# A hybrid decoder layer on one core: mixer outputs loaded straight into the output projection's operand

## The chip, the cores and the metric

The kernel runs on one core of a Trainium2 chip. The metric is device time in microseconds (us). The engines are TensorE (PE, with its weight loads as PEld), VectorE (DVE), ScalarE (ACT), GpSimd (POOL) and SyncE (SP), whose queue issues nearly all DMAs.

## The reference

One layer over a sequence of 512 tokens of width 2048, in float32:

```python
h = _rmsnorm(x, norm_w[l])
p = h @ w_in[l]                       # 2048 x 7824
...
y_a = _rwkv7_mix(...)                 # 16 heads of 64: 1024 columns
y_b = _moba_mix(q_b, k_b, v_b, g_b)   # 4 heads of 128: 512 columns
y_c = _gla_mix(...)                   # 4 heads of 128: 512 columns
mix = jnp.concatenate([y_a, y_b, y_c], axis=-1)
x = x + mix @ w_out[l]                # 2048 x 2048
return _rmsnorm(x, final_norm_w)
```

## The kernel before

**Products in three parts.** Each float32 operand of a projection is split into a rounded high part and the rest: ScalarE copies it to `hi`, VectorE subtracts to get `lo`. A product is then three matmuls, `hi*hi`, `lo*hi` and `hi*lo`. The activations are held in 16 pairs of tiles, `hT[k]`, named `hhi0` to `hhi15` and `hlo0` to `hlo15`, each 128x512.

**The input projection** goes through 62 jobs (`wdad` to `mg3`), each of four units of 12 matmuls with 512 columns (the job `low` is one unit). Unit g of a job reads `hT[4g]` to `hT[4g+3]`. The last job, `mg3`, accumulates in bank `gb1`. Weights come in tiles of 256 KB through three buffers, `raw0` to `raw2`, and are split into four slots, `hi0` to `hi3` and `lo0` to `lo3`. A load may go into a raw buffer when VectorE has split what was in it.

**Side work** (the three mixers) is written as coroutines. `pump` resumes them between the matmuls of the projection by a clock that the program keeps while it is being written; `force` resumes them until a flag is set. Their small matmuls use the banks `sb0` to `sb3`, and their copies and sums stand in the queues of ScalarE and VectorE between the splits. Each finished mixer output is a 128x512 tile, a "mix"; there are 16, and each is written to its own DRAM tensor `mix0` to `mix15`.

**The output projection** has 64 units: four column blocks `cb` of 512 columns, and in each 16 blocks n of w_out, taken in the order `K_ORDER`. Unit (cb, n) multiplies the mix `K_ORDER[n]` by a 128x512 tile of w_out: four row groups `tb` of three matmuls, 12 in all. In the first column block the mixes have to come back from DRAM. Before, they stand in the list `items` between the w_out tiles: mix, w_out, mix, w_out. Each goes through a raw buffer of its own turn (`load`, L1067), and is split from there into `hT[n]` (`split`, L1107), which the input projection has finished with by then. Column blocks 1 to 3 load w_out alone.

The residual input `x` is loaded by `load_x` in four DMAs per column block, in the first three when block n = 8 begins. In the first column block, three row groups of blocks 0 and 1 are done before the fourth, since the fourth needs bank `gb1`, which VectorE must first empty (`f4<-gb1`).

Of the kernel before, what the change touches and what calls it, by code (L numbers as in the profile page):

```python
# [9 lines left out]
F32 = mybir.dt.float32  # L10
F32R = mybir.dt.float32r
I32 = mybir.dt.int32
AF = mybir.ActivationFunctionType
ALU = mybir.AluOpType
# [3 lines left out]
KT = D // 128  # L18
# [31 lines left out]


JOBS = [(n, first_column(n)) for n in ORDER.split()]
N_FIRST = 3
NGB = 4
SKEW = (0, 5, 12, 30)
# [37 lines left out]
def tile_hybrid(ctx: ExitStack, tc: tile.TileContext, x, xT, wu, wlow, wout, par, cst, w2a2_d, aup_d, fw, out):  # L93
    nc = tc.nc
# [179 lines left out]
    Xd = dram.tile([32, 32, 32], F32, name="Xd")  # L274
    mixd = [dram.tile([128, S], F32, name=f"mix{k}") for k in range(KT)]
    mix_ready = [False] * KT


    sides = []
# [429 lines left out]
    def group_norm(q):  # L709
        yield flag(f"y{q}")  # L710
        ysq = ARBf[:, 0:1024]
        y = Yqf.rearrange("p (g n) -> p g n", n=C)
        red(gn[:, 0], y)
        ts(gn[:, 0], gn[:, 0], 1.0 / C, None, ALU.mult)
        tt(y, y, gn[:, 0, :, None].to_broadcast([128, 16, C]), ALU.subtract)
        yield None
        act(ysq, Yqf, AF.Square)
        yield None
        red(gn[:, 1], ysq.rearrange("p (g n) -> p g n", n=C))
        yield None  # L720
        yield from rsqrt(gn[:, 1], gn[:, 2], 1.0 / C, GN_EPS)
        tt(y, y, gn[:, 2, :, None].to_broadcast([128, 16, C]), ALU.mult)
        yield None
        for j in range(2):
            pr = 2 * q + j
            b = yield from bank()
            for cp in range(4):
                tr(sbk[b][:, cp * 128:(cp + 1) * 128], Yq[:, cp, j * 128:(j + 1) * 128])
            u = ARBf[:, 1024 + S * j:1024 + S * j + S]
            act(u, sbk[b], AF.Identity, bias=col(P_LB, pr), scale=col(P_LW, pr))  # L730
            release(b)
            yield None
            tt(u, u, bv[j], ALU.add)
            yield flag(f"ga{pr}")
            tt(u, u, sgt[j], ALU.mult)
            yield None
            dma(mixd[pr], u, nc.sync)
            mix_ready[pr] = True
            yield None
        flags[f"finish{q}"] = True  # L740

# [60 lines left out]
    def gla(g):  # L802
# [114 lines left out]
        for i in range(2):  # L917
            h = 2 * g + i
            sg = fb[5 + i]
            yield flag(f"gg{h}")  # L920
            b = yield from bank()
            for w in range(4):
                tr(sbk[b][:, w * 128:(w + 1) * 128], t3(fo[i])[:, w])
            stt(fo[i], sbk[b], col(P_GN), sg, ALU.mult, ALU.mult)
            release(b)
            yield None
            dma(mixd[12 + h], fo[i], nc.sync)
            mix_ready[12 + h] = True
            yield None


    def moba(h):
        sc = 128 ** -0.5
        yield from evac(f"mq{h}", fb[0])
        yield from evac(f"mk{h}", fb[1])
        n_done = [0]

        def window(w, p, pT):

            n = 128 * (w + 1)  # L940
            sm = small[:, 32 + 4 * w:36 + 4 * w]
            b = yield from bank()
            mm(sbk[b][:, :n], fb[0][:, 128 * w:128 * w + 128], fb[1][:, :n])
            yield None
            tt(sbk[b][:, n - 128:n], sbk[b][:, n - 128:n], causal, ALU.add)
            red(sm[:, 0:1], sbk[b][:, :n], ALU.max)
            ts(sm[:, 1:2], sm[:, 0:1], -sc, None, ALU.mult)
            yield None
            act(p[:, :n], sbk[b][:, :n], AF.Exp, bias=sm[:, 1:2], scale=sc, accum=sm[:, 2:3])
            release(b)  # L950
            yield None
            ck.add("dve", 0.1)
            nc.vector.reciprocal(sm[:, 3:4], sm[:, 2:3])
            ts(p[:, :n], p[:, :n], sm[:, 3:4], None, ALU.mult)
            yield None
            b = yield from bank()
            for i in range(w + 1):
                tr(sbk[b][:, 128 * i:128 * i + 128], p[:, 128 * i:128 * i + 128])
            act(pT[:, :n], sbk[b][:, :n], AF.Copy)
            release(b)  # L960
            yield flag(f"mv{h}")
            b = yield from bank()
            for i in range(w + 1):
                mm(sbk[b][:, 0:128], fb[3][:, 128 * i:128 * i + 128], pT[:, 128 * i:128 * i + 128],
                   start=(i == 0), stop=(i == w))
            vcopy(fb[7][:, 128 * w:128 * w + 128], sbk[b][:, 0:128])
            release(b)
            yield None
            n_done[0] += 1

        def windows(ws, p, pT):
            for w in ws:
                yield from window(w, p, pT)

        spawn(f"m{h} even", windows((0, 2), fb[5], fb[6]))
        yield from evac(f"mv{h}", fb[2])
        b = yield from bank()
        for w in range(4):
            tr(sbk[b][:, w * 128:(w + 1) * 128], fb[2][:, w * 128:(w + 1) * 128])
        act(fb[3], sbk[b], AF.Copy)  # L980
        release(b)
        yield None
        flags[f"mv{h}"] = True
        spawn(f"m{h} odd", windows((1, 3), fb[2], att.rearrange("p a t -> p (a t)")))
        yield lambda: n_done[0] == 4
        yield flag(f"mg{h}")
        tt(fb[7], fb[7], fb[4], ALU.mult)
        yield None
        dma(mixd[8 + h], fb[7], nc.sync)
        mix_ready[8 + h] = True  # L990
        yield None

    def moba_gate(h):
# [13 lines left out]
            flags[f"moba{h}"] = True  # L1007


    K_ORDER = [0, 1, 12, 13, 2, 3, 14, 15, 8, 9, 4, 5, 10, 6, 7, 11]  # L1010
    items, units = [], []
    index = {n: i for i, (n, _) in enumerate(JOBS)}
    tile_no = {n: i for i, n in enumerate([n for n, _ in JOBS if n != "low"])}
# [18 lines left out]
    n_in = len(units)  # L1032
    for cb in range(4):
        for n in range(KT):
            if cb == 0:
                items.append(("mix", n))
            add_unit(("out", cb, n))
    item_of, slot_of, nth, last_in_slot = {}, {}, 0, []
    for i, (kind, n) in enumerate(items):
        if kind == "w":  # L1040
            item_of[n] = i
        if kind in ("w", "mix"):
            slot_of[i] = nth
            nth += 1
            last_in_slot.append(i)
# [21 lines left out]
    def load(i):  # L1067
        kind, n = items[i]
        dep = 0.0
        if kind == "x":  # L1070
            o, src = xraw[n], xT[128 * n:128 * n + 128]
        else:
            slot = slot_of[i]
            o = raws[slot % NRAW]
            if slot >= NRAW:
                dep = split_end[last_in_slot[slot - NRAW]]
            if kind == "mix":
                k = K_ORDER[n]
                force(lambda: mix_ready[k], f"mix {k}")
                src = mixd[k]  # L1080
            else:
                u = units[n]
                if u[0] == "in":
                    src = wu[tile_no[u[1]] * 4 + u[2]]
                elif u[0] == "low":
                    o, src = o[:, 0:KT * 16], wlow
                else:
                    k = K_ORDER[u[2]]
                    src = wout[128 * k:128 * k + 128, 512 * u[1]:512 * u[1] + 512]
        nc.sync.dma_start(o, src)  # L1090
        ck.t["dma"] = max(ck.t["dma"], dep) + 0.75
        load_end[i] = ck.t["dma"] + 2.0

    def square(n, r):

        if n == 0:
            act(fb[0], r, AF.Square)
        else:
            e = act(fb[1 + n % 3], r, AF.Square)
            late_adds.append((n, e))  # L1100
        while late_adds and (len(late_adds) > 2 or n == KT - 1):
            m, e = late_adds.pop(0)
            ck.add("pool", 1.25, e + 0.2)
            nc.gpsimd.tensor_tensor(fb[0], fb[0], fb[1 + m % 3], op=ALU.add)  # L1104
            squares[0] = m + 1

    def split(i):  # L1107
        kind, n = items[i]
# [11 lines left out]
        if kind == "w" and units[n][0] == "low":  # L1120
            v = wl2[:, 0:KT * 32].rearrange("p (k s n) -> p k s n", k=KT, s=2)
            rv = r[:, 0:KT * 16].rearrange("p (k n) -> p k n", k=KT)
            hi, lo, r = v[:, :, 0], v[:, :, 1], rv
        elif kind == "mix":
            hi, lo = hT[n]
        else:
            hi, lo = slot(n)
        e = act(hi, r, AF.Copy, dep=dep)
# [67 lines left out]
    for u in range(n_in):  # L1196
# [22 lines left out]
        unit_end[u] = ck.t["pe"]  # L1219
        if g == 3 or kind == "low":  # L1220
            jobs[n].done, jobs[n].end = True, ck.t["pe"]


    ys = [BKf, BKtf, VSf, ARBf]
# [19 lines left out]

    oldest = [gb[(n_started + i) % NGB] for i in range(NGB)]
    waiting = [bank_job[(n_started + i) % NGB] for i in range(NGB)]
    for cb in range(3):
        banks = oldest if cb % 2 == 0 else sbk
        order = [(n, tb) for n in range(KT) for tb in range(4)]
# [3 lines left out]
        for i, (n, tb) in enumerate(order):  # L1253
            u = n_in + cb * KT + n
            if tb == 0 and not (cb == 0 and n == 1):
                begin(u)
            if cb == 0 and n == 0:
                wait_free(waiting[tb])
            if n == 8 and tb == 0:
                if cb == 0:  # L1260
                    force(lambda: not sides, "side work")
                    nc.gpsimd.dma_start(fwt, fw.rearrange("(o d) -> o d", o=1).to_broadcast([128, D]))
# [97 lines left out]
```

## Time and profile before

| what | value |
|---|---|
| median of 3 runs | 1063.88 us (1063.74 to 1065.58) |
| profiled execution, device time | 1066.24 us |
| its span, first to last instruction | 1064.5 us |
| TensorE busy | 1039.1 us, 98% |
| VectorE, ScalarE busy | 63%, 42% |
| mean granted TensorE clock | 0.992 |

The profiled execution is one more execution, taken with the profiler on. Its device time is 1.74 us more than its span. In the trace `gb` and `sb` are the two groups of PSUM banks, and buffer numbers are left out: `hi` is any of the four slots, `raw` any of the three buffers, `f` any of eight work tiles.

### The profile page before, as it was taken

The page shows a single profiled execution, that of the slowest core. Times are in us where ns is not written, and L with a number is a line of the kernel's source. Part 1 is how long each engine was busy: PE and PEld are TensorE (multiplying, and loading weights), DVE is VectorE, ACT ScalarE, POOL GpSimd, SP SyncE. Part 2 cuts the span into 40 slices and gives each one's busy share as a digit, 9 for nine tenths or more (in the row PEclk, how much of TensorE's full clock was granted, in tenths as well). Part 3 has the DMA queues.
Part 4 walks back from the last instruction along what each step waited for, and adds up shares of the span by engine and source line. Part 5 has one row for each costly group of instructions (what it writes and reads, how often), then busy time and mean ns, then how long its engine had stood idle before and what let it go on. Part 6 is the DMA issues. An engine that isn't in the chain of part 4 may idle for free.

```text
span 1064.5 us, 16752 instructions
## 1 busy us (share of the span) xinstructions
PE 1039.1 (98%) x6376; PEld 819.9 (77%) x6376; DVE 667.2 (63%) x1346; ACT 443.7 (42%) x789; POOL 71.9 (7%) x73
## 2 busy tenths in 40 slices
PE   7799999999999999999999999999999999899996
PEld 5587888767788887778888777888877778688885
DVE  6646659657757775576788665667955654434343
ACT  6464543342554443235534513545322354423333
POOL 4500000000100000010000001000000100102020
PEclk9899999999999999999999999999999999999999
DMA  7232333412232342223333222333341345543534
GB/s 250 94 96 79 91 93 95 110 55 84 80 114 81 100 116 77 77 75 114 97 97 104 75 70 71 98 90 101 104 105 50 83 156 165 162 158 97 161 119 158
DMA packets 80400, 111.87 MB, mean 105 GB/s; under 512 B 28208, under 2 KB 29424, under 8 KB 80192
## 3 DMA queue, kind: packets, MB, share of 16 engines
q1 hardware_dynamic: 80176, 109.76, 34.9%
q8 instruction: 50, 0.82, 0.3%
q0 software_dynamic: 144, 1.05, 0.3%
q14 instruction: 30, 0.25, 0.1%
HBM read 98.62 MB, written 12.16 MB: 104 GB/s over the span
## 4 chain that ended last, share of the span: by engine, by line
PE 90%; DMA 3%; ACT 2%; POOL 2%; issue 2%; DVE 1%; SPq 0%; ACTq 0%; POOLq 0%
PE gb L120 68%; PE sb L116 11%; PE sb L120 9%; PE sb L125 2%; DMA raw<-in_wout_dram 2%; POOL f L1104 2%; DMA raw<-mix 1%; ACT hi L173 1%; ACT hhi L173 1%; DMA BK<-Xd 0%; DVE hlo L133 0%; DMA raw<-in_wu_dram 0%; DVE lo L133 0%; ACT f L173 0%; SPq L1243 0%
## 5 line engine op out<-in xcount | busy, mean ns | idle before, releaser
L120 PE MATMUL gb<-hhi,hi 128*128 128x512 f32 x976 | 403.9, 414 | 5.7 <-ACT hi L173 5.7
L120 PE MATMUL gb<-hhi,lo 128*128 128x512 f32 x976 | 383.3, 393 | 1.0 <-DVE lo L133 1.0
L120 PE MATMUL gb<-hlo,hi 128*128 128x512 f32 x976 | 382.9, 392 | 0.3 <-DVE hlo L139 0.3
L173 ACT ACTIVATE hi<-raw 128x512 fp32r<-128x512 f32 x296 | 186.0, 630 | 391.0 <-PE gb L120 273.3
L133 DVE TENSOR_TENSOR lo<-raw,hi 128x512 fp32r<-128x512 f32 x296 | 212.6, 722 | 209.3 <-ACT hi L173 201.9
L120 PEld LDWEIGHTS gb<-hhi,hi 128*128 128x128 f32 x976 | 184.2, 189 | 49.9 <-ACT hi L173 5.9
L120 PEld LDWEIGHTS gb<-hhi,lo 128*128 128x128 f32 x976 | 184.1, 189 | 42.2 <-DVE lo L133 2.1
L120 PEld LDWEIGHTS gb<-hlo,hi 128*128 128x128 f32 x976 | 184.6, 189 | 34.5 <-DVE hlo L139 1.4
L133 DVE TENSOR_TENSOR scr<-scr 64x30 f32<-64x30 f32 (+14 forms) x240 | 77.5, 323 | 7.2
L120 PE MATMUL gb<-hi,hhi 128*128 128x512 f32 x128 | 50.9, 398 | 2.6 <-ACT hi L173 2.6
L120 PE MATMUL gb<-lo,hhi 128*128 128x512 f32 x128 | 50.7, 396 | 0.2 <-DVE lo L133 0.2
L120 PE MATMUL gb<-hi,hlo 128*128 128x512 f32 x128 | 50.3, 393 | 0.0
L173 ACT ACT_TABLE_LOAD x34 | 43.6, 1283 | 1.0 <-DVE VS L153 0.4
L153 DVE COPY VS<-sb 64x128 f32<-64x128 f32 x64 | 18.5, 289 | 32.7 <-PE sb L116 31.7
L363 POOL TENSOR_TENSOR gn<-gn,mhalf 128x16 f32<-128x16 f32 (+1 forms) x5 | 13.0, 2603 | 309.5 <-DVE gn L149 309.5
L173 ACT ACTIVATE Lt<-sb 64x256 f32<-64x256 f32 (+1 forms) x64 | 19.3, 326 | 33.1 <-PE sb L116 30.5
L173 ACT ACTIVATE f<-sb 64x256 f32<-64x256 f32 (+3 forms) x52 | 17.2, 362 | 35.6 <-PE sb L125 19.2
L120 PE MATMUL sb<-lo,hhi 128*128 128x512 f32 x80 | 31.2, 390 | 0.0
L120 PE MATMUL sb<-hi,hhi 128*128 128x512 f32 x80 | 31.2, 389 | 0.0
L120 PE MATMUL sb<-hi,hlo 128*128 128x512 f32 x80 | 31.2, 389 | 0.0
L120 PEld LDWEIGHTS gb<-hi,hhi 128*128 128x128 f32 x128 | 24.4, 191 | 8.3 <-ACT hi L173 3.3
L120 PE MATMUL sb<-late,hhi 128*128 128x512 f32 x96 | 30.2, 395 | 0.0
(228 smaller groups left out, 1142.9 us busy)
## 6 DMA issues: line engine op xcount, KB each, us to landing
raw<-in_wu_dram SPq DMA_DIRECT2D x244, 256.0 KB
raw<-in_wout_dram SPq DMA_DIRECT2D x64, 256.0 KB
raw<-mix SPq DMA_DIRECT2D x16, 256.0 KB
f<-in_x_dram SPq DMA_DIRECT2D x16, 256.0 KB
Ld<-Lt SPq DMA_DIRECT2D x4, 512.0 KB
mix<-f SPq DMA_DIRECT2D x8, 256.0 KB
mix<-ARB SPq DMA_DIRECT2D x8, 256.0 KB
AW<-in_xT_dram SPq DMA_DIRECT2D x6, 256.0 KB
```

Of the source, the lines that this page charges most:

```text
L116: nc.tensor.matmul(o, l, r, start=start, stop=stop)
L120: nc.tensor.matmul(o, l, r, start=start, stop=stop)
L125: nc.tensor.transpose(o, i, ident[:k, :k])
L133: nc.vector.tensor_tensor(o, a, b, op=op)
L153: nc.vector.tensor_copy(o, a)
L173: nc.scalar.activation(o, a, f, **kw)
L363: nc.gpsimd.tensor_tensor(r, v, mhalf[:, 0:n], op=ALU.pow)
L1104: nc.gpsimd.tensor_tensor(fb[0], fb[0], fb[1 + m % 3], op=ALU.add)
```

## The change

- Mixes leave the list `items` and no longer use raw buffers. A mix is loaded from DRAM straight into the tile `hlo[n]` of the operand (`fetch_mixes`); `place_mixes` then copies it to `hhi[n]` on ScalarE and subtracts in place on VectorE.
- The loads are written into SP's queue earlier. After each of the four units of the last input job, up to four more mixes are fetched, as far as they are ready, and the rest during the first column block.
- A mix that is finished after the input projection was written (here mix 11, the last) does not go to DRAM: it is split from the tile it was computed in (`mixed`).
- `load_x` of the first column block may wait until the side work is done, up to block 13.

```diff
+    def mixed(k, u):
+        if projected_all[0]:
+            hi, lo = hT[K_ORDER.index(k)]
+            act(hi, u, AF.Copy)
+            tt(lo, u, hi.bitcast(F32), ALU.subtract)
+            direct.add(k)
+        else:
+            dma(mixd[k], u, nc.sync)
+        mix_ready[k] = True
...
-            dma(mixd[pr], u, nc.sync)
-            mix_ready[pr] = True
+            mixed(pr, u)
...
     for cb in range(4):
         for n in range(KT):
-            if cb == 0:
-                items.append(("mix", n))
             add_unit(("out", cb, n))
...
-            if kind == "mix":
-                k = K_ORDER[n]
-                force(lambda: mix_ready[k], f"mix {k}")
-                src = mixd[k]
...
+    def fetch_mixes(upto):
+        while fetched[0] < upto and mix_ready[K_ORDER[fetched[0]]]:
+            n = fetched[0]
+            if K_ORDER[n] not in direct:
+                nc.sync.dma_start(hT[n][1].bitcast(F32), mixd[K_ORDER[n]])
+                ck.t["dma"] = max(ck.t["dma"], ck.t["pe"]) + 0.75
+                mix_end[n] = ck.t["dma"] + 2.0
+            fetched[0] += 1
+
+    def place_mixes(must, may):
+        cur, ck.cur = ck.cur, None
+        while placed[0] < KT:
+            n = placed[0]
+            k = K_ORDER[n]
+            if n <= must:
+                force(lambda: mix_ready[k], f"mix {k}")
+                fetch_mixes(n + 1)
+            elif n > may or n >= fetched[0] or mix_end.get(n, 0.0) > ck.t["pe"]:
+                break
+            if k not in direct:
+                hi, lo = hT[n]
+                e = act(hi, lo.bitcast(F32), AF.Copy, dep=mix_end[n])
+                tt(lo, lo.bitcast(F32), hi.bitcast(F32), ALU.subtract, dep=e + 0.2)
+            placed[0] += 1
+        ck.cur = cur
...
-        elif kind == "mix":
-            hi, lo = hT[n]
...
+        if u >= n_in - 4:
+            fetch_mixes(4 * g + 4)
+            place_mixes(-1, KT)
+    projected_all[0] = True
...
                 begin(u)
+                if cb == 0:
+                    fetch_mixes(KT)
+                    place_mixes(n + 1, n + 6)
...
-            if n == 8 and tb == 0:
+            if tb == 0 and n >= 8 and x_loaded < cb + 1 and (cb or not sides or n == KT - 3):
+                x_loaded += 1
```

The instructions of all engines stand as before up to the last input units; the differences lie between there and the end of the first column block. Two places follow.

The queue of SP at the end of the input projection, before: `raw<-in_wout` rows are w_out blocks 0, 1, 2, 3 and 4, `raw<-mix` the mixes between them, and `mix<-ARB` two mixes written out.

```order
L1090 DMA raw0_97<-in_wout_dram 128x512
L179 DMA mix6_180<-ARB_127 128x512
L1090 DMA raw1_98<-mix1_175 128x512
L1090 DMA raw2_99<-in_wout_dram 128x512
L1090 DMA raw0_97<-mix12_186 128x512
L1090 DMA raw1_98<-in_wout_dram 128x512
L1090 DMA raw2_99<-mix13_187 128x512
L1090 DMA raw0_97<-in_wout_dram 128x512
L179 DMA mix7_181<-ARB_127 128x512
L1090 DMA raw1_98<-mix2_176 128x512
L1090 DMA raw2_99<-in_wout_dram 128x512
```

The same place after the change; the first row is w_out block 1, block 0 standing just ahead of it in the place of the first mix.

```order
L1093 DMA raw0_97<-in_wout_dram 128x512
L181 DMA mix6_180<-ARB_127 128x512
L1117 DMA hlo0_66<-mix0_174 128x512
L1117 DMA hlo1_68<-mix1_175 128x512
L1117 DMA hlo2_70<-mix12_186 128x512
L1117 DMA hlo3_72<-mix13_187 128x512
L1093 DMA raw1_98<-in_wout_dram 128x512
L1117 DMA hlo4_74<-mix2_176 128x512
L1117 DMA hlo5_76<-mix3_177 128x512
L1117 DMA hlo6_78<-mix14_188 128x512
L1117 DMA hlo7_80<-mix15_189 128x512
L1093 DMA raw2_99<-in_wout_dram 128x512
```

Four mixes now stand ahead of w_out block 2 (`raw1`) and eight ahead of block 3 (`raw2`), where before each block had one more mix ahead of it. Behind the last row come four mixes, block 4, the write of mix 7, three mixes, and blocks 5 to 13; the loads of `x` stand behind block 13.

ScalarE over the first output blocks, before: `f2`, `f6` and `att` are steps of the last MoBA head, `hi` rows are splits of w_out, `hhi` rows of mixes.

```order
L173 ACTIVATE hi2_102<-raw2_99 128x512
L173 ACTIVATE f2_151,small_160<-sb1_166,small_160 128x512
L173 ACTIVATE hhi2_69<-raw0_97 128x512
L173 ACTIVATE hi3_103<-raw1_98 128x512
L173 ACTIVATE hhi3_71<-raw2_99 128x512
L173 ACTIVATE hi0_100<-raw0_97 128x512
L173 ACTIVATE f6_155<-sb3_168 128x384
L173 ACTIVATE att_157<-sb0_165 128x512
```

The same place after the change.

```order
L175 ACTIVATE f2_151,small_160<-sb1_166,small_160 128x512
L175 ACTIVATE hhi1_67<-hlo1_68 128x512
L175 ACTIVATE hhi2_69<-hlo2_70 128x512
L175 ACTIVATE hhi3_71<-hlo3_72 128x512
L175 ACTIVATE hi3_103<-raw1_98 128x512
L175 ACTIVATE f6_155<-sb3_168 128x384
L175 ACTIVATE hhi4_73<-hlo4_74 128x512
L175 ACTIVATE hhi5_75<-hlo5_76 128x512
L175 ACTIVATE hhi6_77<-hlo6_78 128x512
L175 ACTIVATE hhi7_79<-hlo7_80 128x512
L175 ACTIVATE hi0_100<-raw2_99 128x512
L175 ACTIVATE att_157<-sb2_167 128x512
```

`f6` moved ahead of the split of w_out block 3 (`hi0`), and `att` now stands behind it and behind four more mixes.

## Rows read from the trace of the kernel before

**Rows 1.** page, part 1: busy time of each engine
```profile
PE 1039.1 (98%) x6376; PEld 819.9 (77%) x6376; DVE 667.2 (63%) x1346; ACT 443.7 (42%) x789; POOL 71.9 (7%) x73
```

**Rows 2.** waits of TensorE, whole span: us in total, times, longest
```profile
PE gb L120 <- ACT hi L173: 8.4, 2, 5.7
...
PE sb L116 <- ACT f L173: 1.0, 1, 1.0
```

**Rows 3.** chain that ended last, 840 to the end: start us, us, what
```profile
866.04 3.36 DMA raw<-in_wout_dram
...
872.62 3.93 DMA raw<-in_wout_dram
...
877.28 0.39 ACT f L173
...
905.29 7.38 DMA raw<-mix
...
924.47 43.52 PE sb L120 x192
967.99 43.52 PE gb L120 x192
```

**Rows 4.** timeline of TensorE, 858 to 925: start us, us, instruction, count
```profile
858.75 0.48 PE L120 MATMUL gb<-hhi,hi 128*128 128x512 f32 x1
...
871.65 0.39 PE L120 MATMUL gb<-hi,hhi 128*128 128x512 f32 x1
...
876.29 0.40 PE L120 MATMUL gb<-hi,hlo 128*128 128x512 f32 x1
...
877.72 0.94 PE L116 MATMUL sb<-f,f 128*128 128x128 f32 x6 [1.03 <-ACT f L173]
...
907.73 0.39 PE L120 MATMUL gb<-hi,hlo 128*128 128x512 f32 x1
...
911.10 0.39 PE L120 MATMUL gb<-hi,hlo 128*128 128x512 f32 x1
...
914.10 0.80 PE L120 MATMUL gb<-hi,hhi 128*128 128x512 f32 x1 [2.61 <-ACT hi L173]
...
917.54 0.39 PE L120 MATMUL gb<-lo,hhi 128*128 128x512 f32 x1
...
924.31 0.39 PE L120 MATMUL sb<-hi,hhi 128*128 128x512 f32 x1
```

**Rows 5.** stretches: us, busy (x), PEclk, DMA share, GB/s
```profile
905.70:908.10 2.40, 2.40 (x12) 1.81 (x10) 0.82 (x2) 0.63 (x1) 0.00 (x0) 1.00 0.88 237
908.10:910.50 2.40, 2.17 (x10) 1.56 (x10) 0.54 (x1) 0.00 (x0) 0.00 (x0) 1.00 0.96 335
914.10:917.50 3.40, 3.40 (x7) 2.43 (x8) 1.27 (x2) 0.50 (x1) 0.00 (x0) 0.50 0.60 172
```

**Rows 6.** timeline of SP's queue: start us, us, issue, count
```profile
856.81 0.33 SPq L1090 DMA_DIRECT2D raw<-in_wout_dram  x1
...
903.35 1.84 SPq L1243 DMA_DIRECT2D f<-in_x_dram  x4
...
945.31 1.85 SPq L1243 DMA_DIRECT2D f<-in_x_dram  x4
```

**Rows 7.** timeline of ScalarE: start us, us, instruction, count
```profile
862.84 1.28 ACT L173 ACT_TABLE_LOAD   x1
...
946.27 0.63 ACT L173 ACTIVATE hi<-raw 128x512 fp32r<-128x512 f32 x1 [2.09 <-PE sb L120]
```

**Rows 8.** page, part 5: the copies into hi, all of them
```profile
L173 ACT ACTIVATE hi<-raw 128x512 fp32r<-128x512 f32 x296 | 186.0, 630 | 391.0 <-PE gb L120 273.3
```

**Rows 9.** timeline of VectorE, around 866
```profile
865.93 0.69 DVE L133 TENSOR_TENSOR lo<-raw,hi 128x512 fp32r<-128x512 f32 x1
866.53 0.69 DVE L133 TENSOR_TENSOR ARB<-ARB,bv 128x512 f32<-128x512 f32 x1
867.13 0.29 DVE L133 TENSOR_TENSOR sb<-sb,consts 128x128 f32<-128x128 f32 x1
```

More of the change, by code (lines that the diff above doesn't have):

```diff
@@ L52 @@
 JOBS = [(n, first_column(n)) for n in ORDER.split()]
+K_ORDER = [0, 1, 12, 13, 2, 3, 14, 15, 8, 9, 4, 5, 10, 6, 7, 11]
 N_FIRST = 3
@@ L276, in tile_hybrid @@
     mix_ready = [False] * KT
+    projected_all, direct = [False], set()
+    def mixed(k, u):
[7 more added lines that the diff above has]
+        mix_ready[k] = True
     sides = []
@@ L926, in gla @@
             yield None
-            dma(mixd[12 + h], fo[i], nc.sync)
-            mix_ready[12 + h] = True
+            mixed(12 + h, fo[i])
             yield None
@@ L988, in moba @@
         yield None
-        dma(mixd[8 + h], fb[7], nc.sync)
-        mix_ready[8 + h] = True
+        mixed(8 + h, fb[7])
         yield None
@@ L1007, in others @@
             flags[f"moba{h}"] = True
-    K_ORDER = [0, 1, 12, 13, 2, 3, 14, 15, 8, 9, 4, 5, 10, 6, 7, 11]
     items, units = [], []
@@ L1041, in tile_hybrid @@
             item_of[n] = i
-        if kind in ("w", "mix"):
+        if kind == "w":
             slot_of[i] = nth
@@ L1076, in load @@
                 dep = split_end[last_in_slot[slot - NRAW]]
-            if kind == "mix":
-                k = K_ORDER[n]
-                force(lambda: mix_ready[k], f"mix {k}")
-                src = mixd[k]
-            else:
[L1082 to L1089, printed above, removed]
+            u = units[n]
+            if u[0] == "in":
+                src = wu[tile_no[u[1]] * 4 + u[2]]
+            elif u[0] == "low":
+                o, src = o[:, 0:KT * 16], wlow
+            else:
+                k = K_ORDER[u[2]]
+                src = wout[128 * k:128 * k + 128, 512 * u[1]:512 * u[1] + 512]
         nc.sync.dma_start(o, src)
@@ L1105, in square @@
             squares[0] = m + 1
+    mix_end, fetched, placed = {}, [0], [0]
+    def fetch_mixes(upto):
[22 more added lines that the diff above has]
+        ck.cur = cur
     def split(i):
@@ L1246, in tile_hybrid @@
     waiting = [bank_job[(n_started + i) % NGB] for i in range(NGB)]
+    x_loaded = 0
     for cb in range(3):
```

## The prediction, on record before the run

> **What bounds the kernel now.** I read the page first: TensorE is busy for 98% of the span [rows 1]. That alone doesn't say that nothing is to be had, because busy time there is modelled and holds slow matmuls too. The view of waits gives what is left: matmuls into `gb` waited 8.4 us for ScalarE's copies in two places, the longest 5.7, so the other about 2.7; and one side step waited 1.0 us for ScalarE [rows 2]. The 5.7 us lie at the start of the kernel, where nothing is changed. The chain of waits tells where the others are. In its last part TensorE goes on without a break, 192 matmuls in 43.52 us and again 192 in 43.52 us [rows 3], which is column blocks 1 and 2 of the output projection: 0.2267 us a matmul. The first column block has the same 192 matmuls, and in the timeline it lasts from 871.65 to 924.31, 52.66 us [rows 4]. So 9.14 us of it are not projection. That is the stage the change touches, and everything behind it is bound by TensorE, so what is won there reaches the end one to one.
>
> From the timeline [rows 4] those 9.14 us come apart as follows, each as the distance of two starts less 0.2267 us for each matmul between them.
> - 876.29 to 877.72: 1.43 less 0.23, **1.20 us**, waiting for ScalarE's `f6`.
> - 907.73 to 911.10: 3.37 less 12 matmuls (2.72), **0.65 us**.
> - 911.10 to 914.10: 3.00 less 0.23, **2.77 us**, waiting for a split of w_out by ScalarE.
> - 914.10 to 917.54: seven matmuls (1.59) took 3.44, **1.85 us** more. The granted clock is 0.50 in this stretch [rows 5], that is the 1.2 GHz level; TensorE had stood still just before.
> - The rest, 2.67 us, are 21 small side matmuls and their restarts. They stay.
>
> Sum of the four: 6.47 us. What caused them is in the chain [rows 3]. A split of w_out waited until 876.6 for a load issued at 872.62 that took 3.93 us, and `f6` stood behind that split on ScalarE until 877.28. At 905.29 a mix was loaded that took 7.38 us, against 3.36 us for a load at 866.04; just ahead of it in the queue stand the four loads of `x`, from 903.35 [rows 6]. While they ran, the DMA engines were busy for 0.88 and 0.96 of the time at 237 and 335 GB/s [rows 5]. Three raw buffers serve two loads for each block of 2.72 us (12 matmuls), so a late load can't be covered.
>
> **The change, part by part.**
>
> *Splits.* The same 16 copies and 16 subtractions remain, from `hlo` instead of `raw`. A subtraction in place isn't new: `ARB<-ARB,bv` takes 0.69 us as `lo<-raw,hi` does, and both let the next start 0.60 us later [rows 9]. Cost nothing. One write and one read of 256 KB (mix 11) go; they were off the path: nothing.
>
> *Raw buffers.* They now carry w_out alone, one load for each block, as in column blocks 1 to 3. There four loads of `x` stand in the queue too, at 945.31 [rows 6], and the next split waits 2.09 us for TensorE and not for a DMA [rows 7], while TensorE keeps its 43.52 us. So a 7.38 us landing behind `x` is hidden in this form, and the 0.65, 2.77 and, if the clock fell because of the pause, the 1.85 us go.
>
> *The mix loads* have a new wait. Each goes into an `hlo` that the last input job still reads. That job starts at 858.75 and the output at 871.65 [rows 4], so its four units begin some 3.2 us apart, and four mixes become free in each: up to about 862, 865, 868.5 and 871.5. SP's queue works in order, so w_out blocks 2, 3 and 4 stand behind them and leave at about 862.5, 866 and 869. Block 3 left at 872.62 before, so it is 6 us earlier in spite of the queue. How soon SP goes on after a matmul isn't in the trace; the nearest, 0.02 to 0.1 us between steps of the chain, is lost in these roundings, and even 1 us for all would be covered (below).
>
> The Trainium skill (DMA: Bandwidth & Descriptors, section Anatomy of one DMA — SWDGE (gpsimd) path) speaks against such loads: it says that the DMA engines never wait for a semaphore, the issuing sequencer does, before it dispatches. By that rule every w_out load is held for the mixes ahead of it. The sum already counts on that order, so by the rule it is the same, and the chance of rival 4 hangs on it; no row of before shows such a wait in this stage.
>
> *Transfers.* From 859 to 866 ten loads of 256 KB go out. At 237 to 335 GB/s [rows 5] each takes 0.8 to 1.1 us, so with 3.36 us for the first and nine more behind it, block 3, the tenth, lands between 869.5 and 872.5; if nothing is in the way, at 869.4. Block 4, with 15 transfers ahead since 859, lands by 874 to 879 and is wanted at about 882.
>
> *Is it in time?* ScalarE: a table load at 862.84 takes 1.28 us [rows 7], then come the SiLU of a gate, one split, a second table load and `f5`, to about 867; behind them six copies, `f2`, `f6`, five copies and `att`. At 0.63 us each [rows 8], an upper bound since they overlap, `f6` ends at about 872.2 and `hi0` of block 3 at about 875.3, `att` at 876. TensorE wants `f6` when nine matmuls of the output are done, about 874, and `att` after 15 matmuls and some 1.2 us of side work, about 876.7. Both are in time; the slack is 1.8 and 0.7 us, or over 1 us with overlap. Block 3 may land 2.5 us later than the worst above before it holds up `att`. VectorE: from 868 to the emptying of `gb1` about 13 rows at 0.60 [rows 9], done at about 877; wanted by the fourth row group at about 878.3. So the 1.20 us go too. Had this cover gone, the loss would be what is late, one to one.
>
> *The last mixes.* Mix 7 is written and read back in SP's queue, and its read waits for the write: 3.4 to 7.4 us by the loads [rows 3]. Blocks 5 and 6 stand behind it. Block 5 then leaves at 874 to 878, lands by 882, and is wanted at 887. Nothing.
>
> *Moved in the order:* `load_x` still comes at block 8, since the side work is done by then. Three transposes stand a few matmuls earlier: nothing.
>
> **Sum.** 6.47 us less about 0.3 for short waits that I can't place, 6.2 us. Of the profiled execution: 1066.24 to 1060.0, span 1064.5 to 1058.3. The median of the runs shown is 2.36 us below the profiled execution. I take the same 6.2 us off it: **1057.7 us**.
>
> **The rivals.**
> 1. *A part stays or comes back in the first five blocks* (ScalarE and VectorE are packed there, with 0.7 to 1.4 us to spare by my reckoning). One of the four terms stays, 0.65 to 2.8 us: 1058.5 to 1060.5. Against it: the splits of w_out no longer wait for loads. Chance 0.22.
> 2. *The pause was smaller without the profiler.* The 2.36 us between profile and median may lie in these stalls; then only about 4.1 us are to be had: 1059.8. Nothing in the trace tells. Chance 0.10.
> 3. *The load of `x` still stalls*: 2.77 and 1.85 us stay, since it was the burst and not the double use of the buffers: gain 1.6 to 1.85, 1062.1, no measurable change. Against it: column block 1, where the same burst costs nothing [rows 6, 7]. Chance 0.06.
> 4. *Slower: SP's queue is held by the mix loads.* If block 3 lands after 875, `att` and with it TensorE wait, one to one, and the clock falls again for about 1.85 us. It decides against the change when it costs more than 6.2 and 2.1 us: block 3 landing after about 881.5, 15 us after it was issued. The longest landing in this stage is 7.38 us [rows 3]. It would give 1066 and more. Chance 0.06.
>
> **How the numbers follow.** The forecast, all four stalls gone, has 0.56; it gives 1056.7 to 1058.7. About 0.2%, 2.1 us, is what a measurement of this kernel can tell from no change, so the border is 1061.75. Forecast and rivals 1 and 2 are faster: 0.88. Rival 3 is the same: 0.06; rival 4 slower: 0.06. The range from 1056.4 to 1061.2 holds the forecast and rivals 1 and 2, and leaves out rivals 3 and 4 and a little of each end.
>
> **What would show it.** The first column block would last about 46.2 us instead of 52.66, with no wait of a `gb` matmul there and no stretch of clock 0.50 in it. SP should issue mix loads from 859 to 872 and block 3 at about 866. ScalarE's `hi` rows behind block 4 should wait for TensorE, not for DMA. Right in time but wrong in mechanism: the wait stays and the clock does not fall. The prediction is wrong if `att` or the emptying of `gb1` holds TensorE by more than 2 us at 876 to 879, if a low clock comes at another place, or if the stalls don't exist outside the profile.

## The result and the profile after

The changed kernel took **1058.98 us** (median of 6 runs, 1058.08 to 1059.79); before, measured beside it, took 1064.73 us (1063.74 to 1065.85, 6 runs). The ratio is **0.9948, interval 0.9938 to 0.9959**: faster by 5.75 us, inside the range and 1.3 us above the forecast. Measured once more (below), the gain was 3.84 us. The profiled execution of after took 1058.42 us.

Page, span, part 1, and of part 5 one group of matmuls of the output projection:

```profile
span 1056.7 us, 16747 instructions
...
PE 1035.9 (98%) x6376; PEld 819.5 (78%) x6376; DVE 666.3 (63%) x1346; ACT 442.9 (42%) x789; POOL 71.9 (7%) x73
...
L122 PE MATMUL gb<-hi,hhi 128*128 128x512 f32 x128 | 50.0, 391 | 0.0
```

As many matmuls as in [rows 1], and the share of busy time says nothing, as before. The last number of the third row is what counts: no `gb<-hi,hhi` matmul waits any more. Waits of TensorE, in total, times, longest:

```profile
PE sb L118 <- POOL f L1107: 6.0, 1, 6.0
PE gb L122 <- ACT hi L175: 5.8, 1, 5.8
PE gb L122 <- DVE lo L135: 0.5, 1, 0.5
```

Of the waits in [rows 2] only the 5.7 us at the start of the kernel are left (5.8 here). The 6.0 us for GpSimd lie there too; the same view of before has them, with 6.0, and [rows 2] doesn't show that row. Chain of waits, 845 to the end, and then two stretches (us, busy of PE, PEld, DVE, ACT, POOL, PEclk, DMA share, GB/s):

```profile
870.16 2.77 PE gb L122 x12
872.93 0.67 PE sb L118 x6
...
876.30 40.17 PE gb L122 x177
916.47 43.52 PE sb L122 x192
959.99 43.52 PE gb L122 x192
```

```profile
860.00:870.00 10.00, 10.00 (x48) 7.88 (x46) 6.87 (x16) 8.96 (x15) 0.00 (x0) 1.00 0.88 265
870.00:916.00 46.00, 46.00 (x214) 38.37 (x213) 22.68 (x39) 19.48 (x33) 0.00 (x0) 1.00 0.49 162
```

All the `DMA raw<-` pieces of [rows 3] are gone from this part of the chain, and TensorE goes through column block 0 without a break at clock 1.00. Its first matmul starts at 870.70 and that of column block 1 at 916.31: 45.61 us, against 52.66 [rows 4]. SP's queue:

```profile
858.21 4.36 SPq L1117 DMA_DIRECT2D hlo<-mix  x4
862.67 0.38 SPq L1093 DMA_DIRECT2D raw<-in_wout_dram  x1
863.14 2.03 SPq L1117 DMA_DIRECT2D hlo<-mix  x4
865.26 0.38 SPq L1093 DMA_DIRECT2D raw<-in_wout_dram  x1
865.74 2.44 SPq L1117 DMA_DIRECT2D hlo<-mix  x4
868.73 0.33 SPq L1093 DMA_DIRECT2D raw<-in_wout_dram  x1
869.41 0.32 SPq L181 DMA_DIRECT2D mix<-ARB  x1
870.09 4.97 SPq L1117 DMA_DIRECT2D hlo<-mix  x3
875.15 18.59 SPq L1093 DMA_DIRECT2D raw<-in_wout_dram  x9
893.79 1.85 SPq L1278 DMA_DIRECT2D f<-in_x_dram  x4
```

Four mixes took SP 4.36 us where four loads of `x` take 1.85: it stood at them, and the next w_out load left behind them. The view of SP's own waits says for what: from 857.5 to 876 these loads waited 5.9 us in six places for TensorE's `gb` matmuls. That agrees with the rule of the Trainium skill (DMA: Bandwidth & Descriptors, section Anatomy of one DMA — SWDGE (gpsimd) path) that the issuing sequencer does the waiting; the section is about GpSimd's path, and here SP's queue shows the same. ScalarE, around the places where `f6` and `att` could have come late, and behind the burst of `x`:

```profile
870.26 0.49 ACT L175 ACTIVATE f<-sb 128x384 f32<-128x384 f32 x1 [0.48 <-PE sb L127]
870.65 2.18 ACT L175 ACTIVATE hhi<-hlo 128x512 fp32r<-128x512 f32 x4
872.73 0.62 ACT L175 ACTIVATE hi<-raw 128x512 fp32r<-128x512 f32 x1
874.07 0.60 ACT L175 ACTIVATE att<-sb 128x512 f32<-128x512 f32 x1 [0.72 <-PE sb L127]
...
900.19 0.63 ACT L175 ACTIVATE hi<-raw 128x512 fp32r<-128x512 f32 x1 [2.09 <-PE gb L122]
...
905.63 0.63 ACT L175 ACTIVATE hi<-raw 128x512 fp32r<-128x512 f32 x1 [2.09 <-PE gb L122]
```

`f6` and `att` wait for TensorE, not for a copy or a load. Behind `x` (893.79) every split waits for TensorE to free a slot, from 900.19 on for 2.09 us, as in column block 1 before [rows 7]: the loads land with time to spare.

### The profile page after: what moved, and what is told of

The parts are those of the page before. It is cut to its first block, busy times and chain, and to the rows that moved or that the text cites. A ratio compares the mean times of both kernels' runs of the same rounds, so it can differ in the third digit from the quotient of the medians.

```text
span 1056.7 us, 16747 instructions
## 1 busy us (share of the span) xinstructions
PE 1035.9 (98%) x6376; PEld 819.5 (78%) x6376; DVE 666.3 (63%) x1346; ACT 442.9 (42%) x789; POOL 71.9 (7%) x73
## 3 DMA queue, kind: packets, MB, share of 16 engines
q0 software_dynamic: 144, 1.05, 0.2%
## 4 chain that ended last, share of the span: by engine, by line
PE 97%; ACT 1%; POOL 1%; issue 0%; DMA 0%; DVE 0%; SPq 0%; ACTq 0%; POOLq 0%
PE gb L122 74%; PE sb L118 11%; PE sb L122 9%; PE sb L127 2%; POOL f L1107 1%; DMA raw<-in_wu_dram 0%; ACT hhi L175 0%; ACT hi L175 0%; DVE lo L135 0%; ACT f L175 0%; ACT pbuf L175 0%; ACT ARB L175 0%; DVE VS L135 0%; ACTq L1396 0%; POOLq L1396 0%
## 5 line engine op out<-in xcount | busy, mean ns | idle before, releaser
L122 PEld LDWEIGHTS gb<-lo,hhi 128*128 128x128 f32 x128 | 24.0, 188 | 5.0
```

What stands on the lines that cost most here:

```text
L122: nc.tensor.matmul(o, l, r, start=start, stop=stop)
```

## The experiments

The runs fall into five sets, each beside the kernel before; the profiled execution of each gives the last three columns. "Stage" is from the first matmul of the last input job to the end of column block 1, which is independent of where three transposes of 0.33 us stand; all three are differences of starts that are read to 0.01 us. Times and ratios are medians.

| kernel | us (before beside it) | ratio, interval | block 0 | block 1 | stage |
|---|---|---|---|---|---|
| before, first profile | – | – | 52.66 | 43.52 | 109.08 |
| before again | 1062.97 (1061.39), one run each | – | 49.70 | 43.52 | 106.12 |
| after | 1058.98 (1064.73) | 0.9948, 0.9938 to 0.9959 | 45.61 | 43.52 | 102.36 |
| after again | 1059.43 (1063.27) | 0.9964, 0.9953 to 0.9976 | 45.62 | 43.52 | 102.37 |
| in turn, held | 1059.36 (1063.92) | 0.9959, 0.9947 to 0.9971 | 45.70 | 43.52 | 102.37 |
| no direct split | 1059.48 (1063.92) | 0.9959, 0.9945 to 0.9973 | 45.62 | 43.52 | 102.37 |
| in turn, not held | 1060.73 (1063.59) | 0.9971, 0.9960 to 0.9982 | 45.70 | 43.52 | 103.68 |
| mixes twice | 1062.44 (1063.92) | 0.9989, 0.9980 to 0.9998 | 47.74 | 43.52 | 104.49 |
| all 14 at once | 1066.51 (1063.59) | 1.0027, 1.0017 to 1.0037 | 45.93 | 43.52 | 109.32 |
| no early fetch | 1067.51 (1063.59) | 1.0037, 1.0024 to 1.0050 | 49.06 | 43.52 | 111.36 |
| `x` at block 10 | 1062.80 (1063.27) | 0.9994, 0.9985 to 1.0002 | 49.08 | 43.74 | 105.71 |
| `x` at block 11 | 1062.25 (1063.27) | 0.9995, 0.9984 to 1.0006 | 48.89 | 44.15 | 105.94 |
| `x` at block 12 | 1063.30 (1063.92) | 0.9994, 0.9985 to 1.0003 | 46.70 | 45.54 | 105.14 |
| `x` at block 15 | 1064.46 (1063.59) | 1.0011, 1.0001 to 1.0021 | 46.47 | 48.10 | 107.47 |

My theory was that mixes and w_out in the same three raw buffers leave the loads no lead, so that the burst of `x` stops TensorE. The rival was that the burst alone does it, so that a later `x` is worth as much.

**In turn, held: the raw buffers alone.** Before, with each mix loaded in its old turn, one for each block, but straight into `hlo`, and held until the input units that read that tile are written. No early fetch, no direct split.

```diff
-        if kind in ("w", "mix"):
+        if kind == "w":
...
+        return kind == "mix" and written[0] < n_in - 3 + n // 4
...
+        elif kind == "mix":
...
+            o, src = hT[n][1].bitcast(F32), mixd[k]
```

> One part alone, mended: each mix keeps its turn in the list, is loaded into hlo and split in place, raw buffers carry w_out alone; a mix is now not written into the queue before the input units that read its tile. No fetch ahead of turn, no direct split. x stays at block 8, ahead of the last mix load. Theory A: no pause in the first column block, all of the gain, ratio to before 0.993 to 0.996. Rival (fetching ahead of turn is needed): a pause of 1 us or more at the first blocks, 0.997 or more. Rival (not sending the last mix through DRAM is what counts): the last mix is late behind x, a pause near block 15.

Stage 102.37, as with the whole change. The ratio, 0.9959, is the upper end of the first interval of the whole change and lies inside the second. The four loads of `x` still stand at block 8, ahead of the last mix, and no matmul of the stage waits. So the separate buffers are the change's whole gain. Here too the first mix leaves during the last input job, but the queue is left as it was, mix and w_out by turns; fetching by fours adds nothing. By this account more raw buffers in the old form should give the same; no run tried it.

**No direct split.** After, with mix 11 through DRAM.

```diff
-    projected_all[0] = True
```

> The changed kernel without the direct split: the last mix goes through DRAM as the others do. Theory A: it is off the path, ratio to before as the changed kernel, 0.994 to 0.996. Rival (direct split matters): 0.997 or more, with a wait near the last blocks.

Stage 102.37: the split from the tile of computation is worth nothing that can be measured.

**No early fetch.** After, without the fetches behind the four units of the last input job.

```diff
-        if u >= n_in - 4:
-            fetch_mixes(4 * g + 4)
-            place_mixes(-1, KT)
```

> The changed kernel without the fetches after the last four input units: all mixes are fetched from the first column block on, where they stand in SP's queue behind w_out blocks 2 to 5. Block 5 can leave only when block 2 is split, about 1.3 us after the last input unit but one, so the first mix leaves at about 870 on the clock of the trace of before, lands 3.4 us later and is split 1.3 us after that: TensorE stands still for about 3 us at the first output block, and with a low clock behind it 4 to 5 us in all. Theory A: ratio to before 0.998 to 1.000, most of the gain is lost at the new place. Rival (the place of the fetch does not matter): as the changed kernel, 0.994 to 0.996.

SP's queue, and TensorE's first matmul that waited:

```profile
869.15 0.33 SPq L1093 DMA_DIRECT2D raw<-in_wout_dram  x1
869.53 10.52 SPq L1117 DMA_DIRECT2D hlo<-mix  x15
880.37 19.81 SPq L1093 DMA_DIRECT2D raw<-in_wout_dram  x7
```

```profile
876.36 0.80 PE L122 MATMUL gb<-hi,hhi 128*128 128x512 f32 x1 [4.26 <-ACT hhi L175]
```

Fifteen loads in one piece, begun as the output begins: 4.26 us of pause, a second one of 1.29, and 6.8 us of low clock. That is 9.0 us of stage more than after, about twice the 4 to 5 expected, and the kernel is slower than before. It gives what rival 4 feared, a late load, by another way. So of the early fetch this much is needed: that the loads don't begin, all together, when the output does.

**Two orders in which TensorE is made to wait.** The first is "in turn" without the hold, the second is after with `fetch_mixes(KT)` in place of `fetch_mixes(4 * g + 4)`. In both, mixes are queued ahead of the last input units that read the same tiles, which then compute on mixes; the second splits mix 7 too from its own tile.

> The kernel before with one part of the change alone: each mix keeps its place in the list, right ahead of its block of w_out, but is loaded straight into hlo and split in place, so that raw buffers carry w_out alone. No early fetch, no direct split of the last mix. Theory A: all of the gain, first column block 45 to 47 us, ratio 0.993 to 0.996. Rival C (the gain is in fetching the mixes before the input projection ends): little of it, a pause of 2 us or more in the first blocks, ratio 0.997 or more. Rival D (the gain is in not sending the last mix through DRAM): nothing, ratio 0.999 to 1.001.

> The changed kernel with 14 mixes fetched in one go after the first unit of the last input job, so that SP's queue is held until TensorE has read the last of their tiles, and w_out blocks 2 and 3 leave at about 872 instead of 862.5 and 866 (mix 7, too, is then split from its tile). This tries the rival of the prediction that ends slower. By the reckoning of the prediction block 2 lands at 875.2 or later, f6 stands behind its split and is 2 us late, att behind block 3 about as much: TensorE waits 2 to 3 us at 874 to 879, with a low clock behind it up to 5 us; ratio to before 0.996 to 0.999. If the hold costs nothing, the ratio is that of the changed kernel, 0.994 to 0.996; if the queue is the danger that the rival made of it, it is 1.002 or more.

TensorE of the first and of the second:

```profile
861.86 0.50 PE L120 MATMUL gb<-hlo,hi 128*128 128x512 f32 x1 [1.04 <-DMA hlo<-mix]
```

```profile
865.57 0.79 PE L122 MATMUL gb<-hlo,hi 128*128 128x512 f32 x1 [4.01 <-DMA hlo<-mix]
```

The second didn't test what its expectation says: written in that order, it isn't SP that waits for TensorE but TensorE for 14 loads, 4.01 us and then 6.8 us of low clock. What it shows is the price of a pause in the last input job, about 7 us of stage. The first has the same fault, 1.04 us, and column block 0 of 45.70 is as good as in after. Its ratio, 0.9971, misses the 0.993 to 0.996 of theory A, but the pause lies in the last input job and not in the first blocks, where rival C puts it.

**Mixes twice.** After, with each of the 15 mixes loaded into `hhi` too, ahead of its load into `hlo`.

```diff
+                nc.sync.dma_start(hT[n][0].bitcast(F32), mixd[K_ORDER[n]])
                 nc.sync.dma_start(hT[n][1].bitcast(F32), mixd[K_ORDER[n]])
```

> The changed kernel with every mix loaded twice, first into hhi, where ScalarE overwrites it, then into hlo: 15 more loads of 256 KB in the same stretch, nothing else changed. It prices the crowd of transfers. By the prediction's figures 18 loads leave before w_out block 3 instead of ten, at 0.8 to 1.1 us each block 3 lands at 876 to 881 on the clock of before instead of 869 to 873, 1 to 5 us after it is wanted: TensorE stands still there and its clock falls, ratio to before 0.997 to 1.002. If the transfers have more room than the prediction said, 0.994 to 0.996 as the changed kernel.

```profile
870.00:880.00 10.00, 9.21 (x51) 7.59 (x51) 8.23 (x17) 7.61 (x13) 0.00 (x0) 1.00 1.05 390
```

```profile
878.18 1.16 PE L118 MATMUL sb<-att,f 128*128 128x128 f32 x8 [0.80 <-ACT att L175]
```

The stretch (first fence) is full of transfers, 390 GB/s at a share of 1.05, against 273 at 0.76 in after, and `att` (second) is late by 0.80 us: the place where the prediction put the least slack. What was late isn't w_out block 3, as the expectation has it: ScalarE waited 0.37, 0.71 and 0.66 us for mix loads whose copies stand ahead of `att`. The clock stayed at 1.00. It costs 2.1 us of stage. So the early fetch fits, but without much room.

**`x` later, and nothing else.** Before, with the four loads of `x` in column block 0 at another block than 8 (here 15; then 12, 11, 10). The same condition places GpSimd's load of the final weight, but in all these kernels that load starts at 848.3 to 850.0 us, so it did not move.

```diff
-            if n == 8 and tb == 0:
+            if n == (15 if cb == 0 else 8) and tb == 0:
```

> The kernel before with one thing moved: the four loads of x of the first column block are issued at block 15 instead of block 8, behind all mix loads. Theory A (mixes and w_out take turns in three raw buffers, so any late load stops TensorE; the burst of x made one late): the pause at blocks 13 to 14 and its low clock go, 0.65 + 2.77 + 1.85 = 5.3 us, the 1.20 us wait for f6 stays; ratio to before 0.995, some 1059.5 us. Rival B (the turn-taking alone is too slow, with or without x): a pause of 2 us or more stays in the first column block and the ratio is 0.998 or more.

> The kernel before with the loads of x of the first column block at block 12 instead of 8. At block 15 the first column block had no pause any more, but the sum with x came too late and TensorE stood still at the next column block instead. At block 12 x still stands behind the last mix load. Theory A (with x out of the way the shared raw buffers are just fast enough, the burst of x ahead of a mix made the pause): no pause in blocks 8 to 15 nor at the next column block, 0.65 + 2.77 + 1.85 = 5.3 us less the 1.2 us at f6 that stays; ratio to before 0.995 to 0.997. Rival (x costs wherever it stands as long as mixes use the raw buffers): 0.999 or more.

> The kernel before with x of column block 0 at weight block 10, ahead of the last mix load. By the theory that a mix load behind x is what stalls, one such load is left (block 8 had three), so it lands late as at block 8 and a pause of 0.5 to 3 us remains in column block 0, which lasts 47.5 to 51 us; ratio 0.996 to 0.999. By the rival that the number of loads behind x does not matter, it stays near 52.7 us; by the rival that only the burst's distance from the start of column block 1 matters, it is near 46.7 us as at block 12.

> The kernel before with the four loads of x of column block 0 at weight block 11 and not 8, right behind the last mix load. By the theory (a mix load held up behind x in raw buffers that it shares with w_out) no load of a mix follows x, so the pause in column block 0 is gone as at block 12 (about 46.7 us). At block 12 the sums that need x were late by about 1.4 us at the start of column block 1; here x leaves a block of 2.7 us earlier, so that pause should be gone too and column block 1 last 43.5 us: in all about 6 us less than before, ratio about 0.995, and the second 128-matmul pause with its low clock absent. By the rival that moving x gains nothing, because its burst of 1 MB costs the same wherever it lies, column blocks 0 and 1 together stay at 92 us or more and the ratio at 0.999 to 1.001.

With `x` at block 15: SP's queue, TensorE at the start of column block 1, and a stretch of it.

```profile
917.69 2.64 SPq L1243 DMA_DIRECT2D f<-in_x_dram  x4
```

```profile
926.76 0.50 PE L120 MATMUL sb<-hi,hhi 128*128 128x512 f32 x1 [1.46 <-ACT hi L173]
...
928.18 0.50 PE L120 MATMUL sb<-lo,hhi 128*128 128x512 f32 x1 [0.92 <-DVE lo L133]
```

```profile
929.20:932.60 3.40, 3.40 (x9) 2.64 (x8) 1.91 (x3) 0.63 (x1) 0.06 (x1) 0.50 0.61 195
```

Column block 0 is whole (46.47), but now the sums that need `x` are late, ScalarE stands at them ahead of the next splits, and TensorE pauses a block later. At 12 the same, with less of it (0.30 and 1.13 us); there the chain also has the w_out load right behind `x`, with 5.27 us. So a place between should do, I thought. With `x` at block 11, from the chain, and at block 10, from the chain:

```profile
911.94 6.14 DMA raw<-in_wout_dram
```

```profile
909.23 6.27 DMA raw<-mix
```

Whatever load stands right behind `x` lands late, here after 6.1 to 6.3 us, a w_out block as well as a mix, and TensorE waits for it: 1.53 us at 918.87 with block 11, 0.98 us at 916.91 with block 10. The expectation for block 11 was wrong, and with it the first form of my theory, in which only the loads of mixes were in danger. By the stage column the four places differ from before again by −1.0 to +1.4 us, while the separate buffers give −3.8. The stage of before itself differs between two profiles, so the medians count for more: they are 0.9994 to 1.0011, where theory had 0.995 to 0.999. So the rival falls too: no place for the burst was found that makes up for the missing lead.

**After again**, beside `x` at blocks 10 and 11.

> The changed kernel without an edit, beside the two kernels in which x alone is moved, on one chip. All theories expect the ratio measured before, 0.994 to 0.996. If moving x to block 11 gains as much, the two lie within 0.15% of each other, and the change's gain is that of any placement in which no late load shares buffers with w_out; if the changed kernel is faster by 0.3% or more, the separate raw buffers give something that the place of x does not, such as the 1.20 us at f6.

Faster than `x` at block 11 by 2.82 us, 0.27%: nearly the 0.3% at which the expectation gives the separate buffers something of their own. Against before 0.9964, just above the expected 0.994 to 0.996: 3.84 us, less than in the first measurement (5.75), with intervals that just overlap.

**Before again**, one more profiled execution of the kernel before.

> The kernel before without an edit, profiled once more. Its first profiled execution took 1066.24 us, more than any other run of it (1062.04 to 1065.85), so the question is whether the pauses of column block 0 are the same in another execution. If the pauses are fixed by the program, column block 0 lasts 52.7 us again, with the low clock behind the 2.8 us pause, and all the difference between executions lies before that stage (a low clock of 6.8 or 10.2 us near the kernel's start). If they depend on how the loads happen to land, column block 0 lasts 48 to 52 us, the pause is shorter, and the clock may stay at 1.00 behind it; the change's gain of 3.8 to 5.8 us between medians is then that of the usual pause.

TensorE, and the chain, of that execution:

```profile
910.78 0.50 PE L120 MATMUL gb<-hi,hhi 128*128 128x512 f32 x1 [0.48 <-ACT hi L173]
...
914.92 0.51 PE L120 MATMUL gb<-hi,hhi 128*128 128x512 f32 x1 [0.63 <-ACT hi L173]
```

```profile
896.30 3.35 DMA raw<-in_wout_dram
899.75 0.64 ACT hi L173
901.02 0.70 DVE hlo L133
904.07 5.29 DMA raw<-mix
909.38 0.64 ACT hhi L173
910.04 0.70 DVE hlo L133
910.76 3.38 DMA raw<-in_wout_dram
```

The second answer: the mix behind `x` landed after 5.29 us and not 7.38 [rows 3], the pauses were 0.48 and 0.63 us and not 2.61 [rows 4], the clock stayed at 1.00, and `f6` was late by 0.27 and not 1.03 us. Column block 0 lasted 49.70 us. For `f6` this is the usual size: the four kernels with `x` moved are the kernel before up to that place, and there it was late by 0.25 to 0.30 us. Behind the burst the DMA engines moved less in the first execution: 237 and 335 GB/s at shares of 0.88 and 0.96 [rows 5], against 323 and 364 at 0.94 and 1.03 in the same two stretches of before again, counted from the first load of `x`. Why, the runs don't show. The chain shows why there is no lead: a load starts when the split before it frees its buffer, the next split waits for that load, and so on through the block.

## Why the prediction was right

- **What bounds, and where the time was:** right. The gain in this stage lies in column block 0, and column block 1 behind it is unchanged (43.52 us).
- **What stays in the stage:** 43.52 and 2.67, 46.19 us; measured 45.61 and the 0.33 of the three transposes that now run ahead of it, 45.94. The 0.3 us left for short waits did not appear.
- **Splits cost nothing:** right by ScalarE's and TensorE's waits in after.
- **Raw buffers carry w_out alone, so the burst is hidden:** right, and the runs make it the cause: this part alone gives the whole stage gain.
- **The mix loads hold SP's queue:** right. After's last job begins at 857.47, 1.28 us earlier than before's; on that clock I had w_out blocks 2, 3 and 4 at 861.2, 864.7 and 867.7, and they left at 862.67, 865.26 and 868.73, 0.5 to 1.5 us later than forecast.
- **In time:** right. `f6` was done at 870.75 and used at 872.76, `att` done at 874.67 and used at 875.25. The slack, 2.0 and 0.6 us, is close to the 1.8 and 0.7 forecast, and the run with mixes twice used it up, at `att` first.
- **Last mixes:** nothing, right for mix 11 (no direct split) and for mix 7: block 5, behind its read, left at 875.15, in the 874 to 878 forecast, and no matmul waited.
- **The sum:** the step that was mis-sized is "I take the same 6.2 us off" the median. Its terms (1.20, 0.65, 2.77, 1.85) are those of one execution. In the other they come to 49.70 less 46.19, 3.5 us, with no low clock.
- **Which size is usual:** the smaller one. Between medians the gain was 5.75 and 3.84 us, and 4.4 to 4.6 for the two kernels with the same stage. The differences of the stage to before again, −3.76 for after, −1.63 for mixes twice, −0.41 for `x` at block 10 and +3.2 for all 14 at once, are near those of the medians (−3.84, −1.48, −0.47, +2.9), and the other kernels of these sets agree to 1.3 us or better; against the first profile all would be 1.6 to 3.3 us off. The granted clock, which the record has for each execution, says the same: every profiled one at 0.995 was without a low clock in the stage, and in the set of after again the executions at 0.995 took 1062.06, 1062.69 and 1063.56 us before and 1059.18 and 1059.43 after. So rival 2, to which I gave 0.10, was right in its size in the later sets: the stalls are usually smaller. Its cause was wrong, for before again had the profiler on too and took 1062.97 us, in the midst of the other executions: the stalls follow how the loads land. That the first 5.75 us came so near to 6.2 is then in part luck. How far the 5.75 of the first set comes from larger stalls there isn't known, since only one of its executions was profiled.
- **Rivals 3 and 4** fell: the burst is hidden, and SP, though held, issued in time. Of rival 1 there is no trace: nothing came back in the first five blocks.

## What to carry to other kernels

Where two streams share a small ring of staging buffers and the chain goes load, split, load, split, the ring can be left without a lead. Here the burst in the same queue became a pause at each of the five places tried, and moving it only moved the pause. A stream whose destination has the right size and type can be loaded into its place and split there, which gives the ring back to the other; see to it that those loads enter the queue neither in one piece just as they are needed nor ahead of the last reader. Profile the old kernel twice before a stall that rests on when a load lands is put down at its full size: here one execution had 6.5 us of it and another 3.5.

## What the runs showed of the hardware

The clock fell to 0.50 (the 1.2 GHz level) behind some pauses and not behind others: for 3.4 us behind 2.61 us of waiting [rows 4], and behind 1.46 and 0.92 us close together (`x` at block 15); for 6.8 us, begun within the pause, with 4.26 and 4.01; not at all behind single waits of 0.80, 1.04, 1.29 and 1.53 us, nor behind 0.30 and 1.13 close together (`x` at block 12). Near the start of the kernel, which nothing here changes, the low clock lasted 6.8 us in some executions and 10.2 in others: the same stretch of after and of before again (PEclk third from the end), 17 us by twice what is missing to 1.00. It doesn't go with the change, since mixes twice had 10.2 and `x` at block 11 had 6.8.

```profile
34.00:51.00 17.00, 11.02 (x44) 8.94 (x43) 10.85 (x13) 4.43 (x8) 8.24 (x9) 0.80 0.28 79
```

```profile
34.00:51.00 17.00, 11.02 (x39) 9.02 (x39) 10.11 (x11) 3.42 (x7) 8.08 (x9) 0.70 0.26 79
```

TensorE was busy for 11.02 of these 17 us, so a longer low clock does not cost its full half: from the 100th to the 150th matmul, over this stretch, before fell behind after by 0.44 us and before again by 1.0. Of the 1.28 us by which after's last job begins earlier than that of before, 0.5 were there ahead of this stretch and 0.94 behind it; all of it lies ahead of the stage and is no part of its gain. A 256 KB load right behind the four of `x` landed after 5.27, 5.29, 6.14, 6.27 and 7.38 us; the other w_out and mix loads that the chains of these kernels show in the same part, from 889 to 935, took 2.60 to 3.95 us.
